# A mixer's first activation table loaded behind the casts of x^T; the last down-projection by column halves in every layer; a norm's last 512 columns at once

## The chip, the core and the metric

The kernel runs on one core of one Trainium2 chip, with all its data in that chip's memory. The metric is the device time of one execution in microseconds, taken as the median of several executions. The core has five engines that run their own instruction streams and wait for each other by semaphores: TensorE (PE) multiplies, VectorE (DVE) and ScalarE (ACT) do elementwise work, GpSimd (POOL) a little of it, SyncE (SP) issues the transfers.

## What is computed

Four layers on 256 tokens of 1024 channels, all float32. Each layer is a token mixer and a dense FFN, each followed by a layer norm over the sum with its own input:

```python
for i in range(4):            # mixers: HGRN2, mLSTM, S5, HGRN2
    h = mixer_i(x)            # x @ w_in, a causal recurrence, ... @ w_out
    x = layernorm(ALPHA * x + h, ln_g[i, 0], ln_b[i, 0])
    gate, up = split(x @ w_gate_up[i])          # hidden width 2816
    h = (silu(gate) * up) @ w_down[i]
    x = layernorm(ALPHA * x + h, ln_g[i, 1], ln_b[i, 1])
```

## The kernel before, in words

**Tokens and splits.** The 256 tokens are two halves `h` of 128, one for each set of partitions. Every float32 operand of a matmul is split into two parts, `hi` (the value rounded by a cast) and `lo` (the rest), and every product is made of three matmuls (`mm3`): hi by hi, and the two mixed ones. Weights come in pieces of 1 MB by SP's queue; for each 128x1024 piece ACT casts `hi` (`halve`, L129) and DVE subtracts `lo` (L130), into eight buffers of each kind, so a cast may have to wait until PE has read an older piece.

**The norm.** `norm` takes one half of the tokens. For n in 0, 1 it adds the residual to a PSUM bank of 512 columns (L225) and takes statistics (L226); then come the aggregate (L227), a small DVE operation on the variance (`rsqrt`, L201) and a power on POOL (L202), which give 1/sigma. The normalized row follows in four chunks of 256 columns: subtract the mean and multiply by gamma (L245), multiply by 1/sigma and add beta (L246), two transposes on PE (L250), and `put_split`: ACT casts the transposed columns into the hi part of x^T (`xx`, L269) and DVE subtracts the lo part (L270). The next projection's matmuls read `xx`; those of a half need that half's casts first. All of a norm's instructions get a high priority.

**The FFN.** `ffn` goes over blocks j of 256 hidden columns: `up` (or `across`, for both halves at once) makes gate and up, ACT applies SiLU (`sg`), DVE multiplies (`hd`, L306), `turn` transposes (L313), `parts` splits into `hh` (ACT, L318) and `hl` (DVE, L319), and `dproj` accumulates the down-projection into two banks `a` of 512 columns for each half. The last block's `dproj` runs for half 0, then, after `up` of half 1, for half 1, and the two norms follow. The next mixer's projection begins with half 0 while half 1's norm is under way.

**Activation tables.** ACT's functions come in tables. `table(name)` loads one when the name differs from the last (L84). It makes the load wait for all activations issued under the table before it (`self.tabled`), and every later activation waits for the load. Copies and casts (L129, L269, L318) are not in that list, so the load can stand anywhere among them.

**The order.** A scheduler sorts each engine's instructions once, when the kernel is built, by dependencies and priorities. On the chip each engine runs its list in order: an instruction that waits holds up all that stand behind it. In the FFN of layer 0 the preparation of the S5 layer (`s5_prepare`, L899 to L980) is mixed in; it brings activations and table loads of its own.

Of the kernel before, what the change touches and what calls it, by code (L numbers as in the profile page):

```python
# [17 lines left out]
P = 128  # L18
# [16 lines left out]
class Trunk:  # L35
    def __init__(self, ctx, tc, aps):
        self.ctx, self.tc, self.nc, self.a = ctx, tc, tc.nc, aps
        mk = lambda name, bufs, **kw: ctx.enter_context(tc.tile_pool(name=name, bufs=bufs, **kw))
        self.const = mk("const", 1)
        self.stage = mk("stage", 3)  # L40
        self.split = mk("split", 8)
        self.xp = mk("xp", 3)
        self.gbp = mk("gbp", 1)
        self.small = mk("small", 4)
        self.ps = mk("ps", 2, space=bass.MemoryType.PSUM)
        self.dram = mk("dram", 1, space=bass.MemoryType.DRAM)
        self.n = 0
        c = self.const
        self.ident = c.tile([P, P], F32, name="ident")
        self.root = c.tile([P, 8], F32, name="root")  # L50
        self.nc.gpsimd.memset(self.root, -0.5)
        self.eps = c.tile([P, 1], F32, name="eps")
        self.nc.gpsimd.memset(self.eps, LN_EPS)
        self.xx = c.tile([P, KD, 2, S], F32R, name="xx")
        self.xh, self.xl = (self.xx[:, :, i] for i in range(2))
        self.x = [None, None]
        self.lb = None
        self.tabled, self.loaded, self.table_name = [], None, None
        self.plan, self.ready, self.staged, self.taken = [], {}, 0, 0

    def uid(self, s):
# [16 lines left out]

    def table(self, name):

        if name == self.table_name:
            return
        self.table_name = name
        p = self.nc.scalar.preload_act_table_set(name).ins  # L84
        dep = mybir.DependencyInfo(mybir.DependencyClass.NoSync, mybir.DependencyReason.DATA)
        for i in self.tabled:
            self.tc.add_manual_dep(p, i.name, dep, reason="table order")
        self.tabled, self.loaded = [], p

    def act(self, *args, **kw):  # L90
        i = self.nc.scalar.activation(*args, **kw).ins
# [126 lines left out]
    def norm(self, h, banks, gb, last=None, perm=False, rev=False):  # L218
        nc = self.nc
        z = self.xp.tile([P, D], F32, tag="x", name=self.uid("x"))  # L220
        st = self.small.tile([P, 2, 6], F32, tag="st", name=self.uid("st"))
        mv = self.small.tile([P, 2], F32, tag="mv", name=self.uid("mv"))
        for n in range(2):
            c = slice(n * 512, (n + 1) * 512)
            nc.vector.scalar_tensor_tensor(z[:, c], self.x[h][:, c], ALPHA, banks[n], ALU.mult, ALU.add)  # L225
            nc.vector.bn_stats(st[:, n, :], z[:, c])  # L226
        nc.vector.bn_aggr(mv, st)  # L227
        if last is not None and h:
            sd, r = (self.small.tile([P, 1], F32, tag=t, name=t, bufs=1) for t in ("sd", "rl"))
            self.table("sqrt_and_others")  # L230
            self.act(sd, mv[:, 1:2], AF.Sqrt, bias=self.eps)
        else:
            r = self.rsqrt(mv[:, 1:2], 1, LN_EPS)
        if last is not None:
            for n in range(2):
                c = slice(n * 512, (n + 1) * 512)
                nc.vector.scalar_tensor_tensor(z[:, c], z[:, c], mv[:, 0:1], gb[:, 0, c], ALU.subtract, ALU.mult)
                if h and n == 0:
                    nc.vector.reciprocal(r, sd)
                nc.vector.scalar_tensor_tensor(z[:, c], z[:, c], r, gb[:, 1, c], ALU.mult, ALU.add)  # L240
                nc.sync.dma_start(last[h * P : (h + 1) * P, c], z[:, c])
            return
        for n in range(4):
            c = slice(n * 256, (n + 1) * 256)
            nc.vector.scalar_tensor_tensor(z[:, c], z[:, c], mv[:, 0:1], gb[:, 0, c], ALU.subtract, ALU.mult)  # L245
            nc.vector.scalar_tensor_tensor(z[:, c], z[:, c], r, gb[:, 1, c], ALU.mult, ALU.add)  # L246
            if n % 2 == 0:
                pt = self.bank("t")
            for k in range(2 * n, 2 * n + 2):
                nc.tensor.transpose(pt[:, (k % 4) * P : (k % 4 + 1) * P], z[:, k * P : (k + 1) * P], self.ident)  # L250
            o = (n % 2) * 256
            self.put_split(pt[:, o : o + 256], 2 * n, h, perm=perm, rev=rev and h == 1)
        self.x[h] = z

    def put_split(self, pt, k0, h, scale=None, perm=False, to=None, rev=False):


        nc = self.nc
        n = pt.shape[1] // P
        src = pt.rearrange("p (k t) -> p k t", k=n)  # L260
        if rev:
            src = src[:, :, ::-1]
        t = slice(h * P, (h + 1) * P)
        oh, ol = (x[:, k0 : k0 + n, t] for x in to or (self.xh, self.xl))
        if perm:
            src = pt.rearrange("p (k c j) -> p k j c", k=n, j=4)
            oh, ol = (x.rearrange("p k (j c) -> p k j c", j=4) for x in (oh, ol))
        if scale is None:
            nc.scalar.copy(oh, src)  # L269
            nc.vector.tensor_tensor(ol, src, oh.bitcast(F32), ALU.subtract)  # L270
        else:
            nc.scalar.activation(oh, src, AF.Copy, scale=scale)
            nc.vector.scalar_tensor_tensor(ol, src, scale, oh.bitcast(F32), ALU.mult, ALU.subtract)


    def ffn(self, i, gb, out=None, perm=False, rev=False, extra=()):
        nc, tc = self.nc, self.tc
        with tc.tile_pool(name=self.uid("ffn"), bufs=2, reuse_waits="tile") as fp:
            down = [[self.bank("a") for _ in range(2)] for _ in range(2)]

            hid, gu, dn, turned, wide = {}, {}, {}, {}, {}
            self.table("silu_and_others")
            extra = list(extra)
            last = NBLK - 1
# [52 lines left out]
            def hidden(h, j, b):  # L337
                src, at = (wide[j, b], h) if (j, b) in wide else (turned[h, j], b)
                return [x[:, at * P : (at + 1) * P] for x in src]

            def dproj(halves, j, mid=None):
                if j == last and i == 3:
                    steps = [(x, y, b) for x, y in ((0, 0), (0, 1), (1, 0)) for b in range(2)]
                    for n in range(2):
                        f = slice(n * 512, (n + 1) * 512)
                        for h in halves:
                            for x, y, b in steps:
                                nc.tensor.matmul(down[h][n], hidden(h, j, b)[x], dn[j][b][y][:, f],
                                                 start=False, stop=(x, y, b) == steps[-1])
                    return  # L350
                turns = [(b, h, n) for b in range(2) for h in halves for n in range(2)]
                for q, (b, h, n) in enumerate(turns):
                    if mid and q == len(turns) // 2:
                        mid()
                    f = slice(n * 512, (n + 1) * 512)
                    wh, wl = dn[j][b]
                    self.mm3(down[h][n], hidden(h, j, b), (wh[:, f], wl[:, f]),
                             j == 0 and b == 0, j == last and b == 1)
# [7 lines left out]
            up((1,), 1, lambda: turn(both, 0))  # L366
            load_dn(0)
            dproj(both, 0)
            gb = gb()
            for j in range(2, last):  # L370
# [863 lines left out]
def plan(layers, ffn):  # L1234

    p = []
    for i in layers:
        j = i // 3
        if i % 3 == 0:
            p += [("w_hg", j, s) for s in (0, 1, 8, 9, 10, 11, 4, 5, 6, 7, 2, 3, 12, 13, 14, 15)] + [("w_ho", j, s) for s in range(4)]  # L1240
        elif i % 3 == 1:
            p += [("w_ml", s) for s in range(4)] + [("ml_gw",)] + [("w_ml", s) for s in range(4, 12)] + [("w_mo", s) for s in range(4)]
        else:
            p += [("w_si", s) for s in range(4)] + [("w_so", s) for s in (0, 2, 1, 3, 4, 6, 5, 7)]
        if ffn:
            gu = lambda b: [("w_gu", i, b, 0), ("w_gu", i, b, 1)]
            dn = lambda b: [("w_dn", i, b)]
            p += gu(0) + gu(1) + dn(0)
            for b in range(2, NBLK):
                p += gu(b) + dn(b - 1)  # L1250
            p += dn(NBLK - 1)
    return p


def trunk(tc, aps, out, layers=range(DEPTH), ffn=True):
    with ExitStack() as ctx:
        t = Trunk(ctx, tc, aps)
        nc = tc.nc
        layers = list(layers)
        t.plan = plan(layers, ffn)  # L1260
        with tc.tile_pool(name="first", bufs=1, reuse_waits="tile") as fp:
            t.warm_up(fp)
# [127 lines left out]
```

## Time and profile before

| | |
|---|---|
| median of 3 runs | 1267.98 us (1267.78 to 1268.33) |
| profiled execution | 1267.33 us, its span 1265.5 us |
| granted TensorE clock, mean | 0.999 |
| busy in the span | PE 1250.9 us, DVE 959.9, ACT 712.3, POOL 40.2 |

The span is what the instructions of the profiled execution cover; 1.83 us of its time lie around it. A matmul of 512 columns is shown with some 0.39 us, but the next one starts 0.233 us after it, since matmuls are pipelined; so a stall is read from the distance of two starts. A row with x2 covers two instructions that follow each other. The bracket at a row's end is the idle time ahead of it, and what ended that.

### The profile page before, as it was taken

Reading aid. Unit: us, or ns where it says so; the run is one execution under the profiler, and the core shown is the slowest. Engines: PE = TensorE matmul, PEld = TensorE weight load, DVE = VectorE, ACT = ScalarE, POOL = GpSimd, SP = SyncE. Lnnn points to the kernel's source line nnn. Section 1 sums busy time; section 2 is a strip of 40 time slices with the busy share of each in tenths; the row PEclk is TensorE's granted clock in tenths of the full one; section 3 lists DMA queues with packets and bytes.
Section 4 is the critical chain, followed back from the end, with each engine's and each line's share of the span. In section 5 each row is a group of like instructions: output and inputs, shape, how many; then the busy total and the mean of one; then the engine's idle time right before and its main releaser. Section 6 shows DMA issues by size and latency. Waiting matters only on the chain.

```text
span 1265.5 us, 20380 instructions
## 1 busy us (share of the span) xinstructions
PE 1250.9 (99%) x7941; PEld 1045.2 (83%) x7941; DVE 959.9 (76%) x1734; ACT 712.3 (56%) x1158; POOL 40.2 (3%) x62
## 2 busy tenths in 40 slices
PE   9999999999999999999999999999999999999997
PEld 7977888888798888888878778888879878888886
DVE  6887899876887799866599797666585887766664
ACT  7755576575467555666443356555458654455551
POOL 0000100000100000000000000000000000000000
PEclk9999999999999999999999999999999999999999
DMA  8733565765373276756467647555545433755540
GB/s 322 285 135 136 177 227 202 277 229 203 120 267 133 100 273 220 241 204 243 167 262 285 251 146 256 197 189 181 196 170 193 158 133 106 279 172 196 186 147 33
DMA packets 46463, 249.93 MB, mean 197 GB/s; under 512 B 5632, under 2 KB 10128, under 8 KB 20000
## 3 DMA queue, kind: packets, MB, share of 16 engines
q1 hardware_dynamic: 46240, 248.55, 54.8%
q8 instruction: 62, 1.02, 0.3%
q14 instruction: 33, 0.27, 0.1%
q0 software_dynamic: 128, 0.09, 0.0%
HBM read 234.99 MB, written 13.63 MB: 196 GB/s over the span
## 4 chain that ended last, share of the span: by engine, by line
PE 93%; DVE 3%; ACT 2%; issue 1%; DMA 1%; POOL 0%; SPq 0%; DVEq 0%; ACTq 0%; POOLq 0%
PE g L189 19%; PE g L159 10%; PE g L161 10%; PE g L160 10%; PE g L192 10%; PE a L159 9%; PE a L160 9%; PE a L161 8%; DVE lo L130 1%; PE t L250 1%; PE t L1142 1%; PE g L1130 1%; PE a L635 1%; PE t L1039 1%; PE a L515 1%
## 5 line engine op out<-in xcount | busy, mean ns | idle before, releaser
L130 DVE TENSOR_TENSOR lo<-w,hi 128x1024 fp32r<-128x1024 f32 x389 | 472.4, 1221 | 111.8 <-ACT hi L129 104.8
L129 ACT CAST hi<-w 128x1024 fp32r<-128x1024 f32 x389 | 406.9, 1051 | 187.1 <-PE a L160 105.0
L189 PE MATMUL g<-xx,hi 128*128 128x512 f32 x1024 | 358.2, 395 | 0.0
L192 PE MATMUL g<-xx,lo 128*128 128x256 f32 x1024 | 267.1, 281 | 0.0
L189 PEld LDWEIGHTS g<-xx,hi 128*128 128x128 f32 x1024 | 186.7, 188 | 34.5
L192 PEld LDWEIGHTS g<-xx,lo 128*128 128x128 f32 x1024 | 192.4, 188 | 10.3
L159 PE MATMUL g<-hi,xx 128*128 128x512 f32 x416 | 168.7, 407 | 3.1 <-ACT xx L269 2.9
L161 PE MATMUL g<-lo,xx 128*128 128x512 f32 x416 | 166.3, 402 | 0.1
L160 PE MATMUL g<-hi,xx 128*128 128x512 f32 x416 | 165.5, 399 | 0.0
L160 PE MATMUL a<-hi,hl 128*128 128x512 f32 x344 | 135.5, 394 | 0.0
L159 PE MATMUL a<-hi,hh 128*128 128x512 f32 x344 | 135.4, 396 | 0.0
L161 PE MATMUL a<-lo,hh 128*128 128x512 f32 x344 | 135.4, 393 | 0.0
L329 ACT COPY sum<-g 128x256 f32<-128x256 f32 x128 | 47.6, 372 | 140.5 <-PE g L189 140.3
L330 DVE TENSOR_TENSOR sum<-g,sum 128x256 f32<-128x256 f32 x128 | 54.2, 424 | 68.8 <-ACT sum L329 68.2
L159 PEld LDWEIGHTS g<-hi,xx 128*128 128x128 f32 x416 | 78.4, 189 | 21.8 <-ACT xx L269 4.7
L161 PEld LDWEIGHTS g<-lo,xx 128*128 128x128 f32 x416 | 78.2, 188 | 18.8 <-DVE lo L130 1.7
L160 PEld LDWEIGHTS g<-hi,xx 128*128 128x128 f32 x416 | 78.5, 189 | 16.2
L161 PEld LDWEIGHTS a<-lo,hh 128*128 128x128 f32 x344 | 64.6, 188 | 15.0
L160 PEld LDWEIGHTS a<-hi,hl 128*128 128x128 f32 x344 | 64.5, 188 | 14.9 <-DVE hl L319 0.3
L159 PEld LDWEIGHTS a<-hi,hh 128*128 128x128 f32 x344 | 64.1, 188 | 13.5 <-ACT hh L318 0.6
L159 PE MATMUL g<-xx,hi 128*128 128x256 f32 x200 | 56.7, 283 | 0.0
L161 PE MATMUL g<-xx,hi 128*128 128x256 f32 x200 | 56.5, 283 | 0.0
(308 smaller groups left out, 1766.9 us busy)
## 6 DMA issues: line engine op xcount, KB each, us to landing
w<-in_w_gu SPq DMA_DIRECT2D x88, 1024.0 KB, 4.9
w<-in_w_dn SPq DMA_DIRECT2D x44, 1024.0 KB, 4.9
w<-in_w_hg SPq DMA_DIRECT2D x30, 1024.0 KB, 4.9
w<-in_w_ml SPq DMA_DIRECT2D x12, 1024.0 KB, 4.9
gb<-in_ln SPq DMA_DIRECT2D x8, 1024.0 KB, 5.1
w<-in_w_ho SPq DMA_DIRECT2D x8, 1024.0 KB, 4.9
w<-in_w_so SPq DMA_DIRECT2D x8, 1024.0 KB, 6.3
ct<-s5ct SPq DMA_DIRECT2D x8, 768.0 KB, 7.5
```

What stands on the lines that cost most here:

```text
L129: self.nc.scalar.copy(hi, x)
L130: self.nc.vector.tensor_tensor(lo, x, hi.bitcast(F32), ALU.subtract)
L159: mm(ps, lh, rh, start=start, stop=False)
L160: mm(ps, ll, rh, start=False, stop=False)
L161: mm(ps, lh, rl, start=False, stop=stop)
L189: whole = lambda: mm(ps, hi[:, c], self.xx[:, k].rearrange("p i t -> p (i t)"), start=k == 0, stop=k == KD - 1)
L192: mm(ps[:, S:], lo[:, c], self.xh[:, k], start=False, stop=False)
L250: nc.tensor.transpose(pt[:, (k % 4) * P : (k % 4 + 1) * P], z[:, k * P : (k + 1) * P], self.ident)
L329: nc.scalar.copy(t, ps[:, S:])
L330: nc.vector.tensor_tensor(t, ps[:, 0:S], t, ALU.add)
L515: nc.tensor.matmul(o, att[:, 2 * h + hd % 2, :], v[:, h, c], start=True, stop=h == 0)
L635: nc.tensor.matmul(pl[rows(c)].rearrange("p (h a t) -> p a h t", h=2, a=2)[:, i], kk[:, i * P + 32 * c : i * P + 32 * c + 32], view(q, i * ...
```

## The change

Three edits. `put_split` notes its casts of x^T (L269), and the first table load behind an FFN's end, which is the next mixer's first one, is ordered behind them, as it was behind the activations already; `ffn` empties the list when it starts. `dproj` runs the last block (j == last) by column halves in every layer, where it did so in layer 3 alone: six matmuls for columns 0 to 511 (hi by hi of both pieces b, then hi by lo, then lo by hi), then six for 512 to 1023. And `norm` takes chunks of 256, 256 and 512 columns in place of four of 256.

```diff
--- before.py
+++ after.py
@@ -55,7 +55,7 @@
         self.xh, self.xl = (self.xx[:, :, i] for i in range(2))
         self.x = [None, None]
         self.lb = None
-        self.tabled, self.loaded, self.table_name = [], None, None
+        self.tabled, self.casts, self.loaded, self.table_name = [], [], None, None
         self.plan, self.ready, self.staged, self.taken = [], {}, 0, 0
 
     def uid(self, s):
@@ -78,14 +78,15 @@
 
     def table(self, name):
 
+
         if name == self.table_name:
             return
         self.table_name = name
         p = self.nc.scalar.preload_act_table_set(name).ins
         dep = mybir.DependencyInfo(mybir.DependencyClass.NoSync, mybir.DependencyReason.DATA)
-        for i in self.tabled:
+        for i in self.tabled + self.casts:
             self.tc.add_manual_dep(p, i.name, dep, reason="table order")
-        self.tabled, self.loaded = [], p
+        self.tabled, self.casts, self.loaded = [], [], p
 
     def act(self, *args, **kw):
         i = self.nc.scalar.activation(*args, **kw).ins
@@ -240,16 +241,15 @@
                 nc.vector.scalar_tensor_tensor(z[:, c], z[:, c], r, gb[:, 1, c], ALU.mult, ALU.add)
                 nc.sync.dma_start(last[h * P : (h + 1) * P, c], z[:, c])
             return
-        for n in range(4):
-            c = slice(n * 256, (n + 1) * 256)
+        for k0, k1 in ((0, 2), (2, 4), (4, 8)):
+            c = slice(k0 * P, k1 * P)
             nc.vector.scalar_tensor_tensor(z[:, c], z[:, c], mv[:, 0:1], gb[:, 0, c], ALU.subtract, ALU.mult)
             nc.vector.scalar_tensor_tensor(z[:, c], z[:, c], r, gb[:, 1, c], ALU.mult, ALU.add)
-            if n % 2 == 0:
+            if k0 % 4 == 0:
                 pt = self.bank("t")
-            for k in range(2 * n, 2 * n + 2):
+            for k in range(k0, k1):
                 nc.tensor.transpose(pt[:, (k % 4) * P : (k % 4 + 1) * P], z[:, k * P : (k + 1) * P], self.ident)
-            o = (n % 2) * 256
-            self.put_split(pt[:, o : o + 256], 2 * n, h, perm=perm, rev=rev and h == 1)
+            self.put_split(pt[:, k0 % 4 * P : (k1 - 1) % 4 * P + P], k0, h, perm=perm, rev=rev and h == 1)
         self.x[h] = z
 
     def put_split(self, pt, k0, h, scale=None, perm=False, to=None, rev=False):
@@ -266,7 +266,7 @@
             src = pt.rearrange("p (k c j) -> p k j c", k=n, j=4)
             oh, ol = (x.rearrange("p k (j c) -> p k j c", j=4) for x in (oh, ol))
         if scale is None:
-            nc.scalar.copy(oh, src)
+            self.casts.append(nc.scalar.copy(oh, src).ins)
             nc.vector.tensor_tensor(ol, src, oh.bitcast(F32), ALU.subtract)
         else:
             nc.scalar.activation(oh, src, AF.Copy, scale=scale)
@@ -279,6 +279,7 @@
             down = [[self.bank("a") for _ in range(2)] for _ in range(2)]
 
             hid, gu, dn, turned, wide = {}, {}, {}, {}, {}
+            self.casts = []
             self.table("silu_and_others")
             extra = list(extra)
             last = NBLK - 1
@@ -339,7 +340,7 @@
                 return [x[:, at * P : (at + 1) * P] for x in src]
 
             def dproj(halves, j, mid=None):
-                if j == last and i == 3:
+                if j == last:
                     steps = [(x, y, b) for x, y in ((0, 0), (0, 1), (1, 0)) for b in range(2)]
                     for n in range(2):
                         f = slice(n * 512, (n + 1) * 512)
```

In the two kernels' lists of instructions PE has as many as before; DVE has 1694 for 1736, three fewer in each of 14 norms; ACT 1147 for 1160, with 14 casts fewer and one table load more (20 for 19). Lines below `table` are one higher in the changed kernel up to the norm: L130 is the weight cast, L131 its subtraction, L226 to L228 the norm's sums and statistics, L246 and L247 its two multiplications, L307, L314, L319 and L320 the FFN's `hd`, transposes, `hh` and `hl`. L269 and L270 keep their numbers.

**Start of layer 2, ACT.** The names: `xx` is x^T, `t_6857` and `t_6870` (before), `t_6833` and `t_6846` (after) hold half 0's transposes, `sg` is half 1's last SiLU of the FFN of layer 1, `hh` its split. Before:

```order
L129 CAST hi_6967<-w_6961 128x1024
L91 ACTIVATE sg_6809<-g_6784 128x256
L84 ACT_TABLE_LOAD
L129 CAST hi_6973<-w_6971 128x1024
L269 CAST xx<-t_6857 128x2x128
L318 CAST hh_6822<-t_6819 128x256
L129 CAST hi_6977<-w_6971 128x1024
L269 CAST xx<-t_6857 128x2x128
L269 CAST xx<-t_6870 128x2x128
L129 CAST hi_7055<-w_7053 128x1024
L269 CAST xx<-t_6870 128x2x128
L129 CAST hi_7059<-w_7053 128x1024
```

and with the change:

```order
L130 CAST hi_6935<-w_6929 128x1024
L92 ACTIVATE sg_6785<-g_6760 128x256
L130 CAST hi_6941<-w_6939 128x1024
L269 CAST xx<-t_6833 128x2x128
L319 CAST hh_6798<-t_6795 128x256
L130 CAST hi_6945<-w_6939 128x1024
L269 CAST xx<-t_6833 128x2x128
L269 CAST xx<-t_6846 128x4x128
L130 CAST hi_7023<-w_7021 128x1024
L130 CAST hi_7027<-w_7021 128x1024
L269 CAST xx<-t_6866 128x2x128 x2
L269 CAST xx<-t_6879 128x4x128
```

The load stood between `sg` and a weight cast, ahead of the first cast of x^T; it now comes behind the last cast of half 1, outside this piece. Half 0's casts are three, two of 2x128 and one of 4x128.

**Start of layer 2, DVE.** From the end of half 0's norm to half 1's `rs` (the small operation from which POOL makes 1/sigma); `x_6881` (before) and `x_6853` (after) are half 1's row. Before:

```order
L130 TENSOR_TENSOR lo_6968<-w_6961,hi_6967 128x1024
L270 TENSOR_TENSOR xx<-t_6857,xx 128x2x128
L270 TENSOR_TENSOR xx<-t_6870,xx 128x2x128
L130 TENSOR_TENSOR lo_6974<-w_6971,hi_6973 128x1024
L225 SCALAR_TENSOR_TENSOR x_6881<-x_4943,a_4991 128x512
L225 SCALAR_TENSOR_TENSOR x_6881<-x_4943,a_4992 128x512
L226 BN_STATS st_6882<-x_6881 128x6 x2
L270 TENSOR_TENSOR xx<-t_6870,xx 128x2x128
L227 BN_AGGR mv_6883<-st_6882 128x2
L130 TENSOR_TENSOR lo_6978<-w_6971,hi_6977 128x1024
L201 TENSOR_SCALAR rs_6889<-mv_6883 128x1
```

and with the change:

```order
L131 TENSOR_TENSOR lo_6936<-w_6929,hi_6935 128x1024
L270 TENSOR_TENSOR xx<-t_6833,xx 128x2x128
L226 SCALAR_TENSOR_TENSOR x_6853<-x_4923,a_4967 128x512
L270 TENSOR_TENSOR xx<-t_6846,xx 128x4x128
L227 BN_STATS st_6854<-x_6853 128x6
L226 SCALAR_TENSOR_TENSOR x_6853<-x_4923,a_4968 128x512
L131 TENSOR_TENSOR lo_6942<-w_6939,hi_6941 128x1024
L227 BN_STATS st_6854<-x_6853 128x6
L131 TENSOR_TENSOR lo_6946<-w_6939,hi_6945 128x1024
L228 BN_AGGR mv_6855<-st_6854 128x2
L131 TENSOR_TENSOR lo_7024<-w_7021,hi_7023 128x1024
L202 TENSOR_SCALAR rs_6861<-mv_6855 128x1
```

Between half 1's first L226 and `rs` there are three subtractions of weights (L131), where between the first L225 and `rs` there was one (L130). The order at the start of layer 3 is the same, with other numbers.

**FFN of layer 0, ACT.** `sg_1943` and `sg_1935` are half 0's second SiLU in it, `sc` and `s5r` belong to the preparation of S5. Before:

```order
L129 CAST hi_1910<-w_1908 128x1024
L129 CAST hi_1914<-w_1908 128x1024
L91 ACT_TABLE_LOAD
L91 ACTIVATE sg_1943<-g_1918 128x256
L129 CAST hi_2021<-w_2019 128x1024
L91 ACTIVATE sg_1972<-g_1947 128x256
L318 CAST hh_1992<-t_1989 128x256
L129 CAST hi_2025<-w_2019 128x1024
L129 CAST hi_2057<-w_2055 128x1024
L129 CAST hi_2061<-w_2055 128x1024
L318 CAST hh_1999<-t_1996 128x256
L911 ACT_TABLE_LOAD
```

and with the change:

```order
L92 ACT_TABLE_LOAD
L92 ACTIVATE sg_1935<-g_1910 128x256
L130 CAST hi_1902<-w_1900 128x1024
L130 CAST hi_1906<-w_1900 128x1024
L130 CAST hi_2013<-w_2011 128x1024
L92 ACTIVATE sg_1964<-g_1939 128x256
L130 CAST hi_2017<-w_2011 128x1024
L130 CAST hi_2049<-w_2047 128x1024
L912 ACT_TABLE_LOAD
L912 ACTIVATE s5r_1825<-sc_2068 128x32
L319 CAST hh_1984<-t_1981 128x256
L319 CAST hh_1991<-t_1988 128x256
```

The table for SiLU and half 0's `sg` stand ahead of two weight casts now, and the load at L912 and `s5r` ahead of both `hh` casts. Four rows further on the changed list has a load at L925 that the list before hasn't.

## Rows read from the trace of the kernel before

**Rows 1.** The page's part 1: busy time, share of the span and instructions of each engine.

```profile
PE 1250.9 (99%) x7941; PEld 1045.2 (83%) x7941; DVE 959.9 (76%) x1734; ACT 712.3 (56%) x1158; POOL 40.2 (3%) x62
```

**Rows 2.** PE's waits over the whole span: engine, tile, line, what released it: us, times, longest.

```profile
PE g L159 <- ACT xx L269: 2.9, 5, 0.7
PE t L250 <- DVE x L246: 0.3, 1, 0.3
```

**Rows 3.** PE timeline at three layer starts: start, us, engine, line, op, operands, wait.

```profile
333.09 0.73 PE L159 MATMUL g<-hi,xx 128*128 128x512 f32 x2 [0.64 <-ACT xx L269]
...
637.36 0.39 PE L161 MATMUL a<-lo,hh 128*128 128x512 f32 x1
638.39 0.50 PE L159 MATMUL g<-hi,xx 128*128 128x512 f32 x1 [0.64 <-ACT xx L269]
...
647.98 0.41 PE L250 MATMUL t<-ident,x 128*128 128x128 f32 x2
648.85 0.49 PE L159 MATMUL g<-hi,xx 128*128 128x512 f32 x1 [0.46 <-ACT xx L269]
...
930.30 0.50 PE L159 MATMUL g<-hi,xx 128*128 128x512 f32 x1 [0.67 <-ACT xx L269]
...
940.81 0.50 PE L159 MATMUL g<-hi,xx 128*128 128x512 f32 x1 [0.46 <-ACT xx L269]
```

**Rows 4.** ACT timeline at the start of layer 2.

```profile
630.13 1.05 ACT L129 CAST hi<-w 128x1024 fp32r<-128x1024 f32 x1 [3.62 <-PE g L160]
...
635.72 1.28 ACT L84 ACT_TABLE_LOAD   x1
637.02 1.05 ACT L129 CAST hi<-w 128x1024 fp32r<-128x1024 f32 x1
```

**Rows 5.** ACT's table loads grouped by form: busy us, mean ns, idle before.

```profile
L84 ACT ACT_TABLE_LOAD x13 | 16.7, 1283 | 0.9 <-PEq L1382 0.7
```

**Rows 6.** DVE timeline at the start of layer 2, two norms.

```profile
634.04 0.15 DVE L201 TENSOR_SCALAR rs<-mv 128x1 f32<-128x1 f32 x1
...
636.14 0.87 DVE L245 SCALAR_TENSOR_TENSOR x<-x,mv,gb 128x256 f32<-128x256 f32 x2
...
645.29 1.17 DVE L130 TENSOR_TENSOR lo<-w,hi 128x1024 fp32r<-128x1024 f32 x1
646.38 0.14 DVE L201 TENSOR_SCALAR rs<-mv 128x1 f32<-128x1 f32 x1
```

**Rows 7.** DVE's subtractions that split weights, by form; the last norm's 512-column operation.

```profile
L130 DVE TENSOR_TENSOR lo<-w,hi 128x1024 fp32r<-128x1024 f32 x389 | 472.4, 1221 | 111.8 <-ACT hi L129 104.8 <-PE t L423 3.2
...
1261.14 1.41 DVE L240 SCALAR_TENSOR_TENSOR x<-x,rl,gb 128x512 f32<-128x512 f32 x2
```

**Rows 8.** ACT, then DVE timeline at the start of layer 3.

```profile
922.07 1.05 ACT L129 CAST hi<-w 128x1024 fp32r<-128x1024 f32 x1 [3.64 <-PE g L160]
...
925.71 0.15 DVE L201 TENSOR_SCALAR rs<-mv 128x1 f32<-128x1 f32 x1
...
938.33 0.15 DVE L201 TENSOR_SCALAR rs<-mv 128x1 f32<-128x1 f32 x1
```

**Rows 9.** ACT, then PE timeline early in the FFN of layer 0.

```profile
157.81 1.28 ACT L91 ACT_TABLE_LOAD   x1
...
163.88 0.36 ACT L318 CAST hh<-t 128x256 fp32r<-128x256 f32 x1
...
159.51 0.38 PE L313 MATMUL t<-ident,hd 128*128 128x128 f32 x2
160.09 0.47 PE L159 MATMUL g<-hi,xx 128*128 128x512 f32 x1 [0.20 <-DVE hd L306]
...
162.96 0.38 PE L313 MATMUL t<-ident,hd 128*128 128x128 f32 x2
163.09 0.47 PE L159 MATMUL g<-hi,xx 128*128 128x512 f32 x1
...
165.95 0.39 PE L159 MATMUL a<-hi,hh 128*128 128x512 f32 x1
```

## The prediction

> **What bounds the kernel now.** I read the busy shares first: PE works in 99% of the span and the two engines beside it in 76% and 56% [rows 1]. So DVE or ACT can matter only where PE stops for them, and the whole of what can be won there is a list of stops. That list is PE's waits. Its largest line is matmuls of the next projection that wait for the casts of x^T, 2.9 us in five waits; transposes that wait for a norm's last multiplication come to 0.3 [rows 2]. Next I looked for the places. The first matmul of a mixer waits 0.64 us at 333.09, 0.64 at 638.39 and 0.67 at 930.30, and the first matmul of half 1 waits 0.46 at 648.85 and 0.46 at 940.81 [rows 3]. These are the starts of layers 1, 2 and 3. A stop costs somewhat more than its bracket says: from 637.36 to 638.39 are 1.03 us where 0.233 is the pace, so 0.80 is lost with a bracket of 0.64; I add 0.17 to each.
>
> **Why PE stops at the first matmul.** At layer 2 ACT runs the table load from 635.72 to 637.00, then a weight cast from 637.02 on [rows 4], and only then the cast of x^T that PE wants at 637.6. All three starts have the load in that place. It takes 1283 ns on average [rows 5]. With it gone from there the cast is ready about 1.3 us earlier, more than the 0.64 that PE waits, so the wait at the first matmul goes. That is 0.81 us (0.64 + 0.17) at layer 1, 0.80 at layer 2 and 0.84 at layer 3, 2.45 in all, if nothing else stops PE behind it.
>
> [...]
>
> **Layer 1.** The gain stays. The order has one weight subtraction between half 1's statistics and `rs` there, and in the trace no wait of half 1's transposes or matmuls shows in that stretch. I take −0.81.
>
> **Layers 2 and 3: what comes next.** Behind half 0's projection PE needs half 1's x^T, and it was late before: PE stood at 648.85 and 940.81 [rows 3]. So PE's earlier arrival is worth nothing unless half 1's norm ends earlier too. That norm is made on DVE, and I laid out DVE's order from half 0's `rs` to half 1's. Before, these stand at 634.04 and 646.38 in layer 2, 12.34 us apart, and DVE is busy in between [rows 6].
>
> - Half 0's `rs` comes earlier. With the column halves the first residual sum can start some 0.9 us sooner, and one weight subtraction stands ahead of `rs` in place of two. It needs the weight cast that runs from 630.13 to 631.18 [rows 4]. I leave that cast where it is, since a buffer that PE releases sets it. The subtraction then starts at 631.2, the next operation 1.1 later, so `rs` at about 632.3, which is 1.7 earlier.
> - More subtractions stand between the two `rs`: six for four. One is 1221 ns long, and the operation behind it starts 1.09 after it (645.29 to 646.38) [rows 6, 7]. That is +2.18.
> - Wider norm operations give back a little. Two operations of 256 columns take 0.87 as a pair, two of 512 take 1.41 [rows 6, 7], so one of 512 adds some 0.67 where two of 256 add 0.80. Two such pairs of half 0 lie in the stretch: −0.26. The subtraction of x^T joined from two to one saves less than 0.1, left out.
>
> Sum for half 1's `rs`: 632.3 + 12.34 + 2.18 − 0.26 = 646.56, against 646.38. So it comes 0.2 later than now although it could start 0.9 sooner. From `rs` to the first matmul of half 1 the path (POOL's power, one multiplication, two transposes, a cast) is unchanged, and layer 2 ends up 0.2 us behind where it was: the 0.80 won at its first matmul turns up as a longer stop at half 1's transposes. In layer 3 the same order stands. The cast ends at 923.12, half 0's `rs` moves from 925.71 to about 924.3, and with the distance to 938.33 of 12.62 [rows 8] the same sum gives 924.3 + 12.62 + 2.18 − 0.26 = 938.84; some 0.1 of that distance looks like idle time, so I take 938.7, which is 0.4 later.
>
> **The FFN of layer 0.** Before, a table load at 157.81 stands ahead of half 0's `sg`, and the transposes of `hd` hold PE: 0.58 us from 159.51 to the next matmul, where the same pair takes 0.13 at 162.96 [rows 9]. In the changed order the load and `sg` stand two weight casts (2.1 us) earlier, so `hd` is ready before PE gets there: −0.45. The same list has one table load more a little later, 1.28 us, and the load at L912 ahead of both `hh`. These were done by 164.24, and their first reader starts at 165.95 [rows 9], or 165.5 after the gain. Laid out by ACT's rows I get the later `hh` by 164.5, so 1.0 is left, about 0.6 after DVE's `hl`. The work that hides the extra load is the up-projection that runs until then. Without that cover it would cost up to 0.7.
>
> **The rest.** The 14 casts, 14 subtractions and 28 multiplications saved elsewhere lie beside PE's work. Norms behind a mixer gave PE only short stops at their first transposes; first chunks are unchanged. The last four transposes stand together now and wait for a multiplication of 512 columns instead of one of 256, some 0.27 later at the most. Half 1 has other matmuls ahead of the readers, so I take nothing, with bounds of ±0.3 in each of six norms. Layer 3's last down-projection had the halves before, so the end stays.
>
> **Sum.** −0.81 + 0.2 + 0.4 − 0.45 = −0.66 us. The profiled execution becomes 1267.33 − 0.66 = 1266.67. The median of the runs is 0.65 above it, so 1267.3.
>
> **Rivals.**
>
> *Everything named is won.* If half 1's norm isn't late in layers 2 and 3 (the six subtractions ahead of `rs` fit into idle time that I don't see), all stops go: 2.9 + 0.3 + 0.2 of waits and 0.17 for each of seven, some 4.6 us, so 1263.4. If only the first matmul's stops and that of FFN 0 go, and half 1 is as late after PE's arrival as before, it is 2.45 + 0.45 = 2.9, so 1265.1. For it speaks that the load stands on the way in all three places; against it that DVE shows no idle time between the two `rs`.
>
> *Slower, by late weights.* The third subtraction ahead of half 1's `rs` belongs to the next weight piece. It needs a cast into a buffer that the last down-projection holds. By column halves both pieces are read until its end, where one was free six matmuls before it. I expect the cast ready by 643.3 and the subtraction's turn at 645.4. From 2.1 us of delay on, each further microsecond stops PE at both layer starts. A delay of one more cast and subtraction there (2.2 us each) gives −0.66 + 4.4 = +3.7, so 1271.7. Against it: ACT has time there, and the casts behind wait for PE, not for a transfer.
>
> *Nothing moves.* If the stop at layer 1 goes over to half 1's norm as well, +0.2 there instead of −0.81, the sum is +0.35, so 1268.3.
>
> *A load that costs twice its row.* If ACT stood still for another 1.3 us behind each load, the extra one in FFN 0 would take 2.6 and `hh` come 0.3 to 0.4 late: 1267.7. The next cast 0.02 us behind the load's end [rows 4] speaks against it; 0.02 of my own sum's chance is its. [...]
>
> **Chances.** My sum 0.62; everything or the larger part won 0.18; slower 0.08; nothing moves 0.12. The measurement of this kernel tells about 0.2%, 2.5 us, from no change: faster than 1265.4 takes in nearly all of the first rival, 0.17; slower than 1270.5 the second, 0.08; within it 0.75. The range leaves out the far end of both: 1264.8 (the first rival's smaller price and 0.3) to 1269.4 (my sum with the bounds of ±0.3 in six norms and 0.3 at the starts).
>
> **What would show it.** Right: no wait of the first matmul near 332, 636.5 and 928.5; the load behind the casts of x^T; half 1's `rs` at most 0.5 us either side of 646.4 less what was won before, that is 0.81 + 0.45 earlier on the clock of the trace; and a longer stop, 1 to 2 us instead of 0.9, at half 1's first transposes of layers 2 and 3. In FFN 0, the transposes of `hd` pass without a wait and ACT has 20 loads in all. Wrong: half 1's `rs` more than 1 us sooner (first rival), a wait of DVE for a weight cast ahead of it (second), or stops in layer 1 that were not there.

## The result

Over 22 executions of each, the changed kernel takes 1270.19 us in the median (1267.91 to 1272.31), the kernel before 1267.97 (1267.32 to 1268.64): a ratio of 1.0016, 95% interval 1.0009 to 1.0022. So it is 2.2 us slower. I had predicted 1267.3, with 1264.8 to 1269.4 as the range; the time lies outside it, on the side that I thought the less likely. Its executions spread over 4.4 us, those of before over 1.3.

The profiled execution of the changed kernel, the page's span and busy times:

```profile
span 1269.4 us, 20313 instructions
...
PE 1254.0 (99%) x7941; PEld 1047.1 (82%) x7941; DVE 955.4 (75%) x1692; ACT 713.1 (56%) x1145; POOL 40.3 (3%) x62
```

To compare with [rows 1]: of the 3.9 us by which the span has grown, 3.1 are busy time of PE, which executes the same matmuls. Busier with the same work means slower work. The mean granted TensorE clock is 0.996, against 0.999 before.

PE's waits over the whole span, the largest that concern this change (us in total, times, longest):

```profile
PE t L251 <- DVE x L247: 2.7, 2, 1.4
...
PE g L160 <- ACT xx L269: 0.9, 2, 0.5
PE g L160 <- ACT hi L130: 0.6, 2, 0.3
```

To compare with [rows 2]: the waits for the casts of x^T fell from 2.9 us in five to 0.9 in two, as I had forecast for the table edit (the column halves alone do it too, as the single edits below show). Waits for the norm's last multiplication rose from 0.3 in one to 2.7 in two.

PE's timeline at the start of layer 2:

```profile
637.28 0.48 PE L160 MATMUL a<-hi,hh 128*128 128x512 f32 x1
...
638.15 0.73 PE L349 MATMUL a<-hi,hh 128*128 128x512 f32 x2
...
641.71 0.39 PE L160 MATMUL g<-hi,xx 128*128 128x512 f32 x1
...
647.05 0.40 PE L162 MATMUL g<-lo,xx 128*128 128x512 f32 x1
648.81 0.41 PE L251 MATMUL t<-ident,x 128*128 128x128 f32 x2 [1.37 <-DVE x L247]
649.68 0.51 PE L160 MATMUL g<-hi,xx 128*128 128x512 f32 x1 [0.46 <-ACT xx L269]
...
650.34 0.64 PE L161 MATMUL g<-hi,xx 128*128 128x512 f32 x1
650.77 0.63 PE L162 MATMUL g<-lo,xx 128*128 128x512 f32 x1
...
654.07 0.39 PE L162 MATMUL g<-lo,xx 128*128 128x512 f32 x1
654.29 0.39 PE L160 MATMUL g<-hi,xx 128*128 128x512 f32 x1
654.52 0.40 PE L161 MATMUL g<-hi,xx 128*128 128x512 f32 x1
```

In place of the 1.03 us step at 638.39 [rows 3] PE goes on from 637.28 to 638.15 and beyond nearly at pace. The mixer's first matmul is now the one at 641.71, since the column halves (L349) have moved it behind the last down-projection. But at half 1's transposes it waits 1.37 us, and 0.46 more for the cast. What follows is new. From 650.34 to 650.77 a matmul takes 0.43 us; at 654.29 the pace is 0.23 again. The same stretch in slices of 1 us (us, then busy us of PE, PEld, DVE, ACT and POOL with instructions, the granted clock, DMA share, GB/s):

```profile
649.00:650.00 1.00, 0.54 (x3) 0.19 (x1) 1.00 (x3) 0.37 (x1) 0.00 (x0) 1.00 1.00 401
650.00:651.00 1.00, 1.00 (x5) 0.67 (x5) 1.00 (x3) 0.37 (x1) 0.00 (x0) 0.75 1.12 451
651.00:652.00 1.00, 1.00 (x6) 0.84 (x5) 1.00 (x3) 0.00 (x0) 0.00 (x0) 0.50 0.98 410
652.00:653.00 1.00, 1.00 (x5) 0.81 (x4) 0.90 (x2) 0.69 (x2) 0.00 (x0) 0.50 1.04 414
653.00:654.00 1.00, 1.00 (x4) 0.81 (x3) 0.60 (x1) 1.00 (x1) 0.00 (x0) 0.55 1.02 428
654.00:655.00 1.00, 1.00 (x6) 0.78 (x5) 0.00 (x0) 0.99 (x2) 0.00 (x0) 1.00 1.02 424
```

The granted clock, the third number from the end, falls from 1.00 to 0.50 for 3.4 us: 0.25 us' worth of clock is missing in the slice from 650, and 0.5, 0.5 and 0.45 in the next three, 1.7 in sum. PE is busy throughout those slices, so no count of waits holds this loss. Layer 3 repeats it:

```profile
942.29 0.41 PE L251 MATMUL t<-ident,x 128*128 128x128 f32 x2 [1.35 <-DVE x L247]
943.16 0.51 PE L160 MATMUL g<-hi,xx 128*128 128x512 f32 x1 [0.46 <-ACT xx L269]
```

There the clock is down from 944 to 947.5. In the kernel before the same two places had stops of 0.46 [rows 3], in layer 3 behind one of 0.33, and none of its slices was below 1.00 before 1261, when PE had done its last matmul.

DVE at the start of layer 2, from half 0's `rs` to half 1's:

```profile
632.83 0.15 DVE L202 TENSOR_SCALAR rs<-mv 128x1 f32<-128x1 f32 x1
...
644.87 1.21 DVE L131 TENSOR_TENSOR lo<-w,hi 128x1024 fp32r<-128x1024 f32 x1
646.00 0.20 DVE L228 BATCH_NORM_AGGREGATE mv<-st 128x2 f32<-128x12 f32 x1
646.12 1.17 DVE L131 TENSOR_TENSOR lo<-w,hi 128x1024 fp32r<-128x1024 f32 x1
647.21 0.15 DVE L202 TENSOR_SCALAR rs<-mv 128x1 f32<-128x1 f32 x1
```

14.38 us between the two, where I had 14.26 and the kernel before 12.34 [rows 6].

### The profile page after: what moved, and what is told of

Read it like the earlier page. It is cut to its first block, busy times and chain, and to the rows that moved or that the text cites. A ratio compares the mean times of both kernels' runs of the same rounds, so it can differ in the third digit from the quotient of the medians.

```text
span 1269.4 us, 20313 instructions
## 1 busy us (share of the span) xinstructions
PE 1254.0 (99%) x7941; PEld 1047.1 (82%) x7941; DVE 955.4 (75%) x1692; ACT 713.1 (56%) x1145; POOL 40.3 (3%) x62
## 4 chain that ended last, share of the span: by engine, by line
PE 92%; DVE 4%; ACT 2%; issue 1%; DMA 1%; POOL 0%; SPq 0%; DVEq 0%; ACTq 0%; POOLq 0%
PE g L190 19%; PE g L160 10%; PE g L162 10%; PE g L193 10%; PE g L161 10%; PE a L160 8%; PE a L161 8%; PE a L162 8%; DVE lo L131 2%; PE a L349 1%; PE t L251 1%; PE t L1143 1%; PE g L1131 1%; PE a L636 1%; DMA first<-in_first 1%
## 5 line engine op out<-in xcount | busy, mean ns | idle before, releaser
L131 DVE TENSOR_TENSOR lo<-w,hi 128x1024 fp32r<-128x1024 f32 x389 | 471.8, 1220 | 117.9 <-ACT hi L130 106.5
L130 ACT CAST hi<-w 128x1024 fp32r<-128x1024 f32 x389 | 406.0, 1051 | 187.8 <-PE a L161 103.9
L160 PE MATMUL a<-hi,hh 128*128 128x512 f32 x320 | 126.5, 395 | 0.0
L162 PE MATMUL a<-lo,hh 128*128 128x512 f32 x320 | 125.9, 393 | 0.0
L161 PE MATMUL a<-hi,hl 128*128 128x512 f32 x320 | 125.5, 392 | 0.0
L162 PEld LDWEIGHTS a<-lo,hh 128*128 128x128 f32 x320 | 60.0, 188 | 14.3
L161 PEld LDWEIGHTS a<-hi,hl 128*128 128x128 f32 x320 | 60.0, 188 | 13.9
L160 PEld LDWEIGHTS a<-hi,hh 128*128 128x128 f32 x320 | 60.0, 188 | 12.2
```

Source lines behind the costliest of these rows:

```text
L130: self.nc.scalar.copy(hi, x)
L131: self.nc.vector.tensor_tensor(lo, x, hi.bitcast(F32), ALU.subtract)
L160: mm(ps, lh, rh, start=start, stop=False)
L161: mm(ps, ll, rh, start=False, stop=False)
L162: mm(ps, lh, rl, start=False, stop=stop)
```

## The experiments

The theory (A): half 1's norm comes too late at the starts of layers 2 and 3, since six weight subtractions stand in DVE's order between half 0's `rs` and half 1's, where four stood; PE's stop there grows from 0.46 us (layer 3: 0.33 + 0.46) to 1.4 + 0.46; and after a stop of that length the clock falls. The rival (B): the clock falls, or time is lost, for another reason, such as the new order of the last down-projection, and the stop costs only itself.

**Take the lateness away.** Weight subtractions get an order dependency on the last `rs` of an FFN's end. `e_hold` skips the first piece after the norm (half 0 needs it at once) and holds the next two; `e_hold1` skips two and holds one.

```diff
 def halve(self, x, hi, lo):
     self.nc.scalar.copy(hi, x)
-    self.nc.vector.tensor_tensor(lo, x, hi.bitcast(F32), ALU.subtract)
+    s = self.nc.vector.tensor_tensor(lo, x, hi.bitcast(F32), ALU.subtract).ins
+    r = self.hold.pop(0) if self.hold else None
+    if r is not None:
+        self.tc.add_manual_dep(s, r.name, dep, reason="weights behind the norm")
...
 # norm, at its end, for half 1 of an FFN; e_hold1: [None] * 4 + 2 * [self.rs]
+    self.hold = [None, None] + 4 * [self.rs]
```

> The changed kernel, with the next pieces' weight subtractions (the three ahead of half 1's rs at the starts of layers 2 and 3, and the one behind them) ordered behind that rs. Theory A (half 1's late norm makes PE stand 1.37 + 0.46 us, and that stop lets the granted clock fall to 0.5 for some 3.3 us): rs comes about 3 us earlier, PE hardly stops, the clock stays at 1.00 in both places, and all stops at the layer starts go: about 1263.5 us. Theory B (the clock falls there for another reason, such as the new order of the last down-projection): the stops go but 0.5 stays in the rows near 650 and 944, about 1266.5.

Measured: 1264.35 us (1263.94 to 1265.83), ratio to the kernel before 0.9973 (0.9962 to 0.9983). DVE, then PE, at the start of layer 2 in it:

```profile
641.72 0.69 DVE L232 BATCH_NORM_STATS2 st<-x 128x6 f32<-128x512 f32 x1
642.45 0.21 DVE L233 BATCH_NORM_AGGREGATE mv<-st 128x2 f32<-128x12 f32 x1
642.69 0.15 DVE L207 TENSOR_SCALAR rs<-mv 128x1 f32<-128x1 f32 x1
```

```profile
644.36 0.39 PE L165 MATMUL g<-hi,xx 128*128 128x512 f32 x1
644.59 0.38 PE L256 MATMUL t<-ident,x 128*128 128x128 f32 x2
644.73 0.48 PE L166 MATMUL g<-hi,xx 128*128 128x512 f32 x1
```

Statistics, aggregate and `rs` follow each other without a weight subtraction, `rs` stands at 642.69 instead of 647.21, and PE runs into half 1's transposes at 644.59 at full pace, before it has even done with half 0. No wait on a cast of x^T or on the norm is left among PE's waits at the starts, and no slice there is below 1.00. This is the version that beats both: 3.5 us under the kernel before, 5.8 under the changed one, with all three edits in it. It lies 0.9 above theory A's figure and 2.2 below B's. But the stop and the half clock go together here, so this run doesn't tell what each of them cost.

> As before it, but only the third subtraction is ordered behind rs, so rs comes some 1.1 us earlier and PE's wait at half 1's transposes is 0.2 to 0.4 us in place of 1.37. Theory A: a stop as short as in the kernel before costs no clock; two waits of 1.1 and two stretches at half clock of 1.65 go from the changed kernel: about 1265. Theory B: only the waits go, about 1268.

Measured: 1267.39 us (1266.36 to 1267.91), ratio 0.9995 (0.9986 to 1.0004). The stops were 0.40 + 0.46 in layer 2 and 0.39 + 0.46 in layer 3, and the clock stayed at 1.00. So one subtraction less, 1.1 us in each place, takes 2.8 us away from the changed kernel and most of its spread. The clock did as theory A says, but the time is nearer to B's 1268 than to A's 1265. One part of the rest shows in the trace: this profile enters layer 2 0.14 us behind the kernel before and leaves the S5 mixer 0.78 behind. At 705.22 PE stops for 0.75 us, waiting for ACT's `ys` (a tile of that mixer), which it doesn't in the kernel before. Why that stop appears wasn't followed up.

**Keep the lateness, fill the stop.** Six small matmuls that read `rs` run ahead of half 1's first transposes, in `e_fill` at layers 2 and 3, in `e_fill_l2` at layer 2 alone.

```diff
+        if h and (perm or rev):        # e_fill_l2: if h and perm
+            pf = self.bank("t")
+            for _ in range(6):
+                nc.tensor.matmul(pf[0:1, 0:P], self.rw, self.ident, start=True, stop=True)
         for k0, k1 in ((0, 2), (2, 4), (4, 8)):
```

> The changed kernel with six small matmuls (128 columns, results not used) that wait for half 1's rs, ahead of its first transposes, in layers 2 and 3 only. The norm comes no earlier; PE has work for most of the time between rs and the transposes. Theory A: the clock stays at 1.00 and about 3.3 us come back although the transposes start when they did: 1267 to 1267.5. If the clock doesn't hang on PE's stop: 1270 to 1270.5.

Measured: 1267.85 us (1266.79 to 1269.39), ratio 1.0000 (0.9991 to 1.0009). PE at the start of layer 2, and the slices behind:

```profile
647.16 1.47 PE L248 MATMUL t<-ident,rs 128*1 128x128 f32 x12
648.56 0.44 PE L256 MATMUL t<-ident,x 128*128 128x128 f32 x2
649.46 0.51 PE L160 MATMUL g<-hi,xx 128*128 128x512 f32 x1 [0.46 <-ACT xx L274]
```

```profile
650.00:651.00 1.00, 1.00 (x7) 0.75 (x8) 1.00 (x2) 0.37 (x1) 0.00 (x0) 1.00 1.07 440
651.00:652.00 1.00, 1.00 (x7) 0.87 (x6) 1.00 (x3) 0.65 (x2) 0.00 (x0) 1.00 0.94 387
652.00:653.00 1.00, 1.00 (x6) 0.78 (x6) 1.00 (x2) 1.00 (x1) 0.00 (x0) 1.00 1.08 436
```

The six matmuls are twelve instructions in the trace. The transposes come at 648.56 and the first matmul at 649.46. Both are 0.2 to 0.3 us sooner than in the changed kernel, but this execution came to layer 2 sooner by 0.37, so the norm gains nothing. Yet the clock stays at 1.00 and 2.3 us return. This is the cleanest of the runs: but for the twelve instructions PE, DVE and ACT execute the same lists in the same order as in the changed kernel. So the two traces can be compared matmul by matmul, and that gives the price of the half clock. The matmul at 654.07 in the changed kernel is this one here:

```profile
652.29 0.40 PE L162 MATMUL g<-lo,xx 128*128 128x512 f32 x1
```

The changed kernel was 0.26 us later at the transposes and is 1.78 later here: 1.5 us of PE's time. In layer 3 the same reckoning gives 1.6 (942.29 against 940.52, then 947.50 against 944.15). Together they are the 3.1 us by which PE's busy time had grown.

> The changed kernel with the six small matmuls in layer 2 only. Theory A: the half clock at layer 2 goes and the one at layer 3 stays, so about half of what both brought (2.4 us) comes back: 1269 us, with the clock at 0.5 in rows near 945 in those executions that have it. If the place doesn't matter and one stop's cure does for both: 1267.8.

Measured: 1268.54 us (1266.84 to 1270.24), ratio 1.0003 (0.9994 to 1.0012). By the medians 1.65 of the 2.3 us belong to layer 2 and 0.7 to layer 3, but the interval is as wide as the difference. In its profiled execution PE stopped 1.36 + 0.46 us in layer 3 and the clock there stayed at 1.00, so layer 3's stop costs the clock in some executions only. Layer 3 is thus a comparison without any filler: the instructions and the stop are the changed kernel's, only the clock differs, and the changed kernel loses 1.6 us to this trace in that stretch.

**The same stop without the change.** `e_wait1` is the kernel before with one repeated pass of half 1's statistics at layers 2 and 3; `e_wait1_fill` adds the six matmuls.

```diff
+        for _ in range(1 if h and (perm or rev) else 0):
+            nc.vector.bn_stats(st[:, 1, :], z[:, 512:])
         nc.vector.bn_aggr(mv, st)
```

> The kernel before, with one more pass of half 1's statistics (the same result again) ahead of its aggregate at the starts of layers 2 and 3; the order also puts one more weight subtraction ahead of rs. Half 1's norm comes 0.6 + 1.1 = 1.7 us later in both places. Theory A: the stop grows and the clock falls as in the changed kernel, 2 x (1.7 + 1.65): about 1274.7 us. If only the wait counts: 1271.4.

Measured: 1272.40 us (1272.27 to 1274.16), ratio 1.0038 (1.0025 to 1.0050): 4.5 us more, between the two forecasts. PE in layers 2 and 3, then slices of both places:

```profile
650.30 0.41 PE L252 MATMUL t<-ident,x 128*128 128x128 f32 x2 [1.81 <-DVE x L248]
651.18 0.80 PE L159 MATMUL g<-hi,xx 128*128 128x512 f32 x1 [0.46 <-ACT xx L271]
...
944.93 0.41 PE L252 MATMUL t<-ident,x 128*128 128x128 f32 x2 [2.05 <-DVE x L248]
945.80 0.50 PE L159 MATMUL g<-hi,xx 128*128 128x512 f32 x1 [0.46 <-ACT xx L271]
```

```profile
651.00:652.00 1.00, 0.82 (x2) 0.56 (x3) 1.00 (x4) 0.12 (x1) 0.00 (x0) 0.50 1.11 447
652.00:653.00 1.00, 1.00 (x6) 0.82 (x5) 1.00 (x3) 0.37 (x1) 0.00 (x0) 0.50 1.03 430
...
946.00:947.00 1.00, 1.00 (x8) 0.83 (x8) 1.00 (x3) 0.17 (x1) 0.00 (x0) 1.00 0.31 131
947.00:948.00 1.00, 1.00 (x7) 0.85 (x6) 1.00 (x2) 0.58 (x2) 0.00 (x0) 1.00 0.08 16
```

Layer 2 fell to 0.50 behind a stop of 1.81 + 0.46 us. Layer 3 stopped for longer, 2.05 + 0.46, and stayed at 1.00. So neither of the changed kernel's new orders is needed for the clock to fall, and a stop of this length doesn't bring it every time: two waits of 1.7 and one half clock of 1.65 would be 5.

> The kernel before with one more pass of half 1's statistics, as above, and the same six small matmuls ahead of half 1's transposes. The change isn't in it. Theory A: the stop's own cost stays and the half clock goes: 1270.8 to 1271.2, where the run without the matmuls had 1272.4. If the clock has nothing to do with PE's stop: 1272.4.

Measured: 1271.96 us (1271.11 to 1272.96). No slice at the two places is below 1.00, but the medians differ by only 0.44 us, less than their spreads, and both forecasts missed. The traces of the pair have the same order too: with the filler the transposes of layer 2 come 0.33 us later, and the matmul that ends the half clock without it (654.34) comes 0.93 sooner (653.41). So 1.3 us return in layer 2 of this execution. The matmuls wait for `rs` themselves here, 0.50 and 0.74 us, which may be why the whole kernel shows less.

**Which edits make half 1 late.** Each edit alone, and the table edit with one other. The number of weight subtractions between the two `rs` at layers 2 and 3 is counted in the instruction lists. Each kernel takes whole hunks of the change's diff, and the last is the kernel before with the diff of `e_hold`. The forecasts, in the order table; halves; chunks; table and halves; table and chunks; `e_hold` on the kernel before:

> The kernel before with the table edit alone. Between half 0's rs and half 1's there are three weight subtractions on DVE at layer 2 and four at layer 3 (four and four before, six and six in the changed kernel). Theory A (the count of subtractions in that stretch sets half 1's norm, its lateness sets PE's stop, a long stop costs the clock): the first matmul's waits go at all three starts, half 1 is no later than before, so no half clock: 1265.5 to 1266.5. If the table edit by itself makes half 1 late (all that PE gains is a longer stop): 1267.9.

> The kernel before with the column halves alone. Four subtractions in the stretch as before, and half 0's rs up to 1.7 us earlier, so half 1's stops shrink or go; the first matmul's waits stay, since the table load does: 1266 to 1267, clock at 1.00. If the halves' own order stops PE: 1268 or more.

> The kernel before with the chunks of 256, 256 and 512 alone. FFN 0's stop goes (0.45 won), five subtractions in the stretch put half 1's rs 0.8 to 1.0 us later at layers 2 and 3, so PE stops there for 1.2 + 0.46: 1269.4 without half clock, up to 1271.5 with it in part of the executions.

> The table edit and the column halves, with four chunks of 256 columns as before. Five subtractions in the stretch, with half 0's rs as early as in the changed kernel, so half 1's rs comes 1.0 us earlier than there. Theory A: a stop of about 0.3 + 0.46 us, no half clock, as in the run where the third subtraction was moved: 1267.2. If the halves alone bring the half clock: 1269 to 1270.

> The table edit and the wider chunks, with the last down-projection as before. Five subtractions, and half 0's rs not earlier than in the kernel before, so half 1's rs is 1 us later than there while PE comes 0.8 earlier: a stop of some 2 us in front of half 1's transposes. Theory A: the clock falls in most executions, about 1270 us. If the stop costs only itself: 1268.2 (0.8 won and 1.0 lost twice, 0.4 won at layer 1 and at FFN 0 each).

> The kernel before with only the order edit of the first experiment: the weight subtractions of the second and third piece behind half 1's rs. Two subtractions in the stretch instead of four. Theory A: half 1's stops (about 1.3 us at layer 2, 1.7 at layer 3) go, those of the first matmuls stay: 1265 to 1265.8. If half 1's norm wasn't what held PE there: 1267.9.

| edits | subtractions, layers 2 and 3 | half 1's stop: wait + cast, us | half clock at these starts, in the profile | median us | ratio to before |
|---|---|---|---|---|---|
| none | 4, 4 | 0 + 0.46; 0.33 + 0.46 | no | 1267.97 | |
| table | 3, 4 | 0 + 0.46; 0.53 + 0.46 | no | 1267.53 | 0.9998 (0.9989 to 1.0006) |
| halves | 4, 4 | 0 + 0.46; 0 + 0.73 | no | 1269.15 | 1.0009 (1.0000 to 1.0018) |
| chunks | 5, 5 | 1.28 + 0.46; 1.31 + 0.46 | layer 2 | 1271.65 | 1.0029 (1.0017 to 1.0040) |
| table, halves | 5, 5 | 0.64 + 0.46; 0.65 + 0.46 | no | 1268.18 | 1.0003 (0.9994 to 1.0012) |
| table, chunks | 5, 5 | 1.98 + 0.46; 1.31 + 0.46 | layer 2 | 1271.01 | 1.0025 (1.0015 to 1.0034) |
| all three | 6, 6 | 1.37 + 0.46; 1.35 + 0.46 | layers 2 and 3 | 1270.19 | 1.0016 (1.0009 to 1.0022) |
| all, `e_hold1` | 5, 5 | 0.40 + 0.46; 0.39 + 0.46 | no | 1267.39 | 0.9995 (0.9986 to 1.0004) |
| all, `e_hold` | 3, 3 | none | no | 1264.35 | 0.9973 (0.9962 to 0.9983) |
| none, `e_hold` | 2, 2 | none | no | 1267.10 | 0.9995 (0.9986 to 1.0004) |

Three readings. The clock fell in every profile with a wait of 1.28 us or more at layer 2's transposes (four of four without filler), in one of five at layer 3, and in none with 0.65 or less. The chunks are the edit that does the most harm: they add a subtraction to the stretch or two, alone or with other edits, and cost 3.7 us alone, 3.5 beside the table edit and 2.0 beside table and halves. With the halves half 0's `rs` comes earlier, which pays part of it back: table and halves have five subtractions too, but stops of 0.64 and 0.65 only, and all three together are better than chunks alone. And the table edit alone, which takes the very wait away that I read first, gives no measurable gain: in layer 3 a stop of 0.53 turns up at half 1, as in the second step of my forecast, and of the 0.68 us that its profile is ahead when layer 2 begins 0.29 are left when the S5 mixer ends, where the 0.75 us wait for `ys` stands again (704.22). All six forecasts were too low: the table edit by 1.0 us, the halves by 2.15, table and halves by 1.0, table and chunks by 1.0, the held kernel before by 1.3, the chunks by 0.15.

The single edits also correct what I read at the first matmuls. With the halves alone they don't wait either, though the load stands ahead of the cast (start of layer 2, ACT):

```profile
638.55 1.28 ACT L84 ACT_TABLE_LOAD   x1
639.85 0.37 ACT L269 CAST xx<-t 128x256 fp32r<-128x256 f32 x1
```

No weight cast stands between the two now, and PE asks for the cast only behind the last down-projection, at 643.88. And with table and chunks, where no load is there, PE still waits 0.80 us at layer 1 and 0.73 at layer 3: two weight casts stand between `sg` and the cast. So the load was one of the things on the way, and either of two edits takes the waits away.

The halves alone still lose. The trace shows where: in layer 1, at a stop that I had not looked for, PE waiting for a weight subtraction:

```profile
344.01 0.49 PE L161 MATMUL g<-lo,xx 128*128 128x512 f32 x1 [1.04 <-DVE lo L130]
```

Behind it is another wait of 0.46. The pair of table and halves has the same stop there; all three edits together don't.

## Why the prediction was wrong

**The step that failed.** "... layer 2 ends up 0.2 us behind where it was: the 0.80 won at its first matmul turns up as a longer stop at half 1's transposes." The stop was there, and in size: half 1's first matmul starts at 649.68 against 648.85, and as the changed kernel's execution was 0.47 late on reaching that layer, the layer itself is 0.36 behind, for a forecast of 0.2; in layer 3 (943.16 against 940.81, 2.02 late on reaching it) 0.33 for a forecast of 0.4. I priced the longer stop as the time that PE stands, and the pace behind it at nothing. It costs more: the clock falls behind it, 1.5 and 1.6 us of PE's time in the two stretches of this execution. So the terms +0.2 and +0.4 of the sum were 1.9 each, of which a later, shorter wait in the S5 mixer gave 0.4 back (0.29 us at 690.07, where the kernel before waits 0.70). Not every execution need pay both: taken over executions the half clock is 2.3 us (`e_fill`), 2.3 of the 2.9 us by which I missed. Without it the changed kernel has the time of the kernel before, within the interval of 0.09% (1.1 us) either way. I had even listed that stop, "1 to 2 us instead of 0.9", among the things to be seen in the profile, and had not asked what the engine does after it. All rows that I had read were at 1.00, and none of mine could price the other level. The runs tie it to PE's stop: the changed kernel and `e_fill` differ in the six matmuls that fill it, the slice from 651 is at 0.50 in the one and at 1.00 in the other, and the medians are 1270.19 and 1267.85 us. Among my rivals one was missing: a stop moved from one place to another isn't neutral if, as in layer 2 here, it comes out as one long stop (1.37 + 0.46 us) in place of two short ones (0.64 and 0.46).

**Right.** The waits at the three starts went. That the table load held PE there was right for the kernel before, where the table edit alone removes them, but the changed kernel didn't need it: the halves alone remove them too. Half 0's `rs` came 1.7 us early, as forecast (632.83 against 634.04, 0.47 late), and the two `rs` are 14.38 us apart for a forecast of 14.26. On the trace's clock half 1's `rs` is at 647.21 where my sign asked for 645.1, give or take 0.5, because the execution reached the layer 0.47 late instead of 1.26 early. DVE sets half 1's norm, and the order, not any duration, decided (`e_hold`). ACT early in FFN 0:

```profile
155.19 1.28 ACT L92 ACT_TABLE_LOAD   x1
156.48 0.39 ACT L92 ACTIVATE sg<-g 128x256 f32<-128x256 f32 x1
...
163.25 1.28 ACT L912 ACT_TABLE_LOAD   x1
...
164.68 0.63 ACT L319 CAST hh<-t 128x256 fp32r<-128x256 f32 x2
...
166.40 1.28 ACT L925 ACT_TABLE_LOAD   x1
```

The load and `sg` now come ahead of the casts, and PE's stop of 0.45 at 160.09 [rows 9] is gone; PE is 0.41 further on behind it. The extra load at 166.40 and the late `hh` at 164.68 held nobody up.

**Mis-sized.** Layer 1: −0.81 forecast; from the last wide matmul of FFN 0 to the first of FFN 1 the changed kernel is 0.37 us faster. The stop itself went, which was worth 0.65; 0.28 of it came back inside the mLSTM mixer, most of it where PE waits 0.18 for DVE at 368.98. That term is 0.4 of the miss.

**The rivals.** "Everything named is won" asked for DVE to have idle time between the two `rs`; it has none, but with the order changed by hand the price that I gave for the larger part won, 1265.1, and for all of it, 1263.4, bracket what `e_hold` reached; as that kernel also lost time in the S5 mixer, the agreement is partly luck. "Slower, by late weights" ended on the right side by the wrong mechanism: the third subtraction was ready in its turn (646.12, right behind the aggregate), no weight was late. "Nothing moves" failed in its condition: layer 1's stop didn't go over to half 1's norm. Nor did a load cost twice its row: `sg` starts 0.01 us behind the load at 155.19.

The profiled execution is 3.9 us longer in its span, more than the medians' 2.2. Some 1.1 of it is lost in the first 14 us, with two short waits (0.28 and 0.34) for casts of the first weights that no edit concerns; the profiles of the other kernels, at 127 us, lie between 0.05 ahead and 1.3 behind.

## What to carry to other kernels

When a stop is moved rather than removed, add it to what already stands where it goes, and ask of PE not only how long it will stand but at what clock it goes on: here 1.37 + 0.46 us in one place cost 1.5 more, while 0.64 and 0.46 at two places had cost only themselves. A busy time that grows for the same instructions (here by 3.1 us), or a matmul pace of 0.43 us for 0.233, is where that shows; no list of waits has it. And where a change only shifts priorities, count on the engine that will be waited for next what now stands ahead of the thing waited for: a few order dependencies on DVE turned 2.2 us lost into 3.5 won.

## What the runs showed of the hardware

After stops of 1.28 to 1.98 us (plus 0.46) at layer 2's transposes the granted clock went to 0.50 for about 3.4 us, with PE busy for nearly all of it, and then back to 1.00; PE lost 1.3 to 1.6 us by it where a trace with the same order and a clock of 1.00 shows the difference. In layer 3 a stop of 2.05 + 0.46 us left it at 1.00 in one kernel, and one of 1.35 + 0.46 brought it down in another, so the length of the stop alone doesn't decide. Which of the two happens differs from execution to execution of one kernel: of the changed kernel's 22, the twelve with a mean clock of 0.995 or 0.996 took 1270.0 to 1272.3 us, the ten with 0.997 or 0.998 took 1267.9 to 1270.3. The mean also holds the kernel's end: in the profile of the kernel before the clock is at 0.50 in the last 3.7 us of the span, in that of the changed kernel in the last 4.5. PE's last matmul has ended by then (at 1258.0 and 1261.8), so this costs PE nothing. What separates layer 3 from layer 2 was not tried.
